# A hybrid SSD and forgetting-attention block: GpSimd's two-input operations on VectorE, h's forms from a float32 copy, a later softplus chain, long output-gate steps, closing sums in PSUM

## The chip, the cores and the metric

The kernel runs on one core of a Trainium2 chip. The core has a matrix engine (TensorE, PE in the profile; PEld are its weight loads), three engines for elementwise work (VectorE or DVE, ScalarE or ACT, GpSimd or POOL), and SyncE (SP), whose queue issues the DMAs here. SBUF is the on-chip memory, PSUM the accumulators that matmuls write (8 banks of 128 x 512 float32). The metric is the device time of one execution in microseconds; a kernel's time is the median of several runs.

## The reference

One decoder layer on x of 1024 tokens by 1024 channels, all float32. c is turned into shift, scale and gate; h is the modulated RMS norm of x; one projection of h gives everything that follows. A Mamba-2 branch (16 heads, chunks of 128 tokens) and a forgetting-attention branch (8 heads of 128) run side by side:

```python
ada = jax.nn.silu(c) @ w_ada + b_ada
shift, scale, gate = jnp.split(ada, 3, axis=-1)
h = _rmsnorm(x, norm_w) * (1.0 + scale[:, None, :]) + shift[:, None, :]
proj = jnp.einsum("bsd,de->bse", h, w_in)
z_ssm, xbc, dt_raw, q, k, v, z_att, f_logit, g_logit = jnp.split(proj, offsets, axis=-1)
y_ssm = _ssd_branch(z_ssm, xbc, dt_raw, conv_w, conv_b, dt_bias, a_log, d_skip, ssm_norm_w)
y_att = _fox_branch(q, k, v, z_att, f_logit, b_f)
g_ssm, g_att = jnp.split(jax.nn.sigmoid(g_logit + b_gate), N_BRANCHES, axis=-1)
merged = g_ssm * (y_ssm @ w_proj_ssm) + g_att * (y_att @ w_proj_att)
x = x + gate[:, None, :] * (merged @ w_out)
return _rmsnorm(x, final_norm_w)
```

`_ssd_branch` runs a causal convolution over 4 tokens and a silu on xbc, takes dt = softplus(dt_raw + dt_bias), and computes the SSD recurrence chunk by chunk. `_fox_branch` is causal softmax attention with a bias from the running sum of log sigmoid(f_logit + b_f), times silu(z_att).

## The kernel before

**Precision.** Every float32 operand of a matmul is split in two: `hi`, its rounding to the type `fp32r`, made by ScalarE, and `lo = raw - hi`, made by a subtraction on GpSimd or VectorE (`split`, L101). A product is three matmuls: hi x hi, hi x lo, lo x hi. `unit` (L87) loads a piece of 128 x 512 weights into a raw tile (tag `wr`, 4 buffers) and splits it into `wh` and `wl` (5 buffers each). GpSimd is the default for the subtraction; a call can name VectorE. Both the cast and the subtraction read the raw tile, which is free for the next load when both are done.

**Strassen products.** Large products of 2 x 2 blocks take seven block products instead of eight (Winograd's form; the products are numbered 1 to 7). Sums of weight blocks are called s1, s2, s4; sums of blocks of h or of the branch outputs are the forms. After each product the block sums x, u2, u3, u4 are built from the PSUM result by adds on VectorE.

**Stages, in the order of the program.** A planner orders the instructions of each engine from the program's order, from priorities and from a model of the machine; each engine then runs its own list in that order, and so does SP with its DMAs.

1. Start (L202 to L326): x and w_ada are loaded; `ada_cols` forms the modulation, `h_half` (L298) transposes x, modulates it (`xa`, L305) and splits it into `hh` and `hl`, held as 8 tiles of 128 x 1024 each. The first three gate slabs (`FIRST`) are multiplied as h comes in.
2. Forms of h (L435): `v_slab(0)` gives the first values and the raw dt and f (`tmp`, a tile of the scratch tag `ev`, 4 buffers of 128 x 1028). `t_forms(k)` for k = 0 to 3 rebuilds h blocks as hh + hl (L440, two on each engine), takes four differences (L441 to L444) and splits them into the tiles tha, tla, thb, tlb. Then `gate_slab(3)`, the softplus chain `dt_chain` (L363) and the prefix sums `ssm_sums` (L401).
3. Pairs (L616): 19 pairs of 128-column slabs, each a Strassen product `c_pair` (L459): 4 raw weight tiles, 4 sums, 7 splits (four into wh and wl, three into `sh` and `sl`), 84 matmuls, 6 adds, and the evacuation of four results by kind: `gate_out` (tanh on ScalarE), `silu_out` (tanh, then a VectorE product), `conv_out` (L528: five VectorE passes over 128 x 1024 for each slab). The table `WPREP` says before which pair the block sums of the closing weights (`w_sums`, L575, stored to DRAM as `ws_scr`) and the output gate's steps (`out_gate`, L548, and `gate_sum`) are done. `out_gate` accumulates w_gate times c into `gb`, one of the `ev` tiles, 256 columns at a time.
4. SSD (L630 to L794): for four groups of four heads, eight chunks each, `ssd_half` (L671) builds the masked decays (`ab`, L686, then `m4`), xd and xe (x times dt, times the decay), the state `st32` with its split `sn`, and the output ys. The list `FILL` puts projections (`v_slab`, `qk_spill`) between as filling for TensorE.
5. Attention (L956 to L1070): for each head `attend` (L993), at high priority, beside `qk_slab` of the next head. GpSimd masks the bias (L1004) and scales the probabilities (L1021). `EARLY` names products of the SSM projection that are done behind heads 6 and 7 (`early`, L924).
6. Closing (L1077 to L1173): the remaining products of the SSM projection (`ps`), seven of the attention projection (`pa`), seven of the output projection (`o`), four tiles each, in the orders `OSSM`, `OATT`, `OOUT`, which are the same. `post` (L866) takes each PSUM tile: in `ps` and `pa` it makes 7 VectorE adds per tile over the seven products, and calls `done` when a block result is complete. In `o`, `pre` (`out_pre`, L1124) adds partial sums to the residual on GpSimd instead. `prod_c` (L897) and `mms` (L1154) issue the matmuls; `bank` hands out PSUM banks, 3 of the tag `mm` and 5 of `pp`. `WV` and `WVI` name the closing weight units that VectorE splits.

GpSimd does most splits, half of L440, two sums in each `w_sums` (L588, L589) and half its products with the gate (L581), xe (L703), the sum of squares (L778), one difference per tile in the closing forms (L861, L1096), the merge of the branches (L1109), the residual sums (L1126), a product with the final weight (L1139), and the powers for the norms.

## Time and profile before

| | |
|---|---|
| median of 3 runs | 1287.4 us (1284.27 to 1290.71) |
| profiled execution, its own time | 1286.09 us |
| its span (first to last instruction) | 1284.4 us |
| mean granted TensorE clock | 0.974 |
| ACT busy | 594.8 us (46%) |
| bytes moved by DMA | 219.70 MB |

In the views below an engine's busy time is the union of its instructions' records. Records of consecutive instructions overlap a little, since an engine's pipe takes the next one in before the last one is out; matmul records overlap their successors by nearly half. A row of the grouped views reads: line, engine, operation, output and inputs by the program's names, partitions x elements, count, then busy us, mean ns of one, idle time of the engine just before, and what ended that idle time. The table by stage cuts the span where the program passes from one stage to the next: 75 the end of the first slabs, 131 the first products of pairs in full, 545 the SSD, 760 mainly attention, 1066 the closing.

### The profile page before, as it was taken

The numbers are of one execution on the slowest core, as the hardware profiler recorded it, in microseconds if no ns is written. First come the engines' busy times: TensorE is split into PE (matmuls) and PEld (weight loads), VectorE is DVE, ScalarE is ACT, GpSimd is POOL, SyncE is SP. The second block draws the span as 40 slices with busy tenths as digits, with TensorE's granted clock in tenths as the row PEclk, the third lists the DMA queues.
The fourth block names the chain that finished last, engine by engine and source line by source line (L and its number), as shares of the span: only waits on it lengthen the run. The fifth ranks groups of instructions, "written<-read, shape, count | busy, mean of one in ns | idle before, by whom it ended". The sixth has DMA issues, their size and how long they took to land. (4 is left out here: it accounts for less than half of the span.)

```text
span 1284.4 us, 18783 instructions
## 1 busy us (share of the span) xinstructions
PE 1183.9 (92%) x6206; PEld 988.8 (77%) x6206; DVE 963.1 (75%) x1618; ACT 594.8 (46%) x1194; POOL 776.1 (60%) x644
## 2 busy tenths in 40 slices
PE   4897899999978999999988999999999999999896
PEld 3686688777766788799778888888887787878685
DVE  6979767787799566348689764545667968999997
ACT  5443324242423232477667733444456553444354
POOL 3258465474755476448887966435446635587666
PEclk9998899998989999999999999999999999999999
DMA  8422443624556566654565558623236619766143
GB/s 346 158 100 98 160 123 124 213 64 167 188 185 216 175 211 228 223 177 148 188 200 163 173 191 296 210 87 116 74 127 210 201 55 328 224 188 193 52 116 145
DMA packets 104126, 219.70 MB, mean 171 GB/s; under 512 B 11818, under 2 KB 19420, under 8 KB 103004
## 3 DMA queue, kind: packets, MB, share of 16 engines
q1 hardware_dynamic: 104028, 218.50, 51.5%
q8 instruction: 49, 0.80, 0.3%
q14 instruction: 49, 0.40, 0.1%
HBM read 154.85 MB, written 63.61 MB: 170 GB/s over the span
## 5 line engine op out<-in xcount | busy, mean ns | idle before, releaser
L103 POOL TENSOR_TENSOR wl<-wr,wh 128x512 fp32r<-128x512 f32 (+1 forms) x188 | 281.5, 1508 | 135.7 <-ACT wh L102 130.7
L102 ACT CAST wh<-wr 128x512 fp32r<-128x512 f32 (+1 forms) x214 | 129.8, 618 | 158.4 <-DMA wr<-w_c 53.7
L103 POOL TENSOR_TENSOR sl<-sr,sh 128x512 fp32r<-128x512 f32 x57 | 91.0, 1603 | 78.8 <-ACT sh L102 65.7
L115 PE MATMUL mm<-hh,wh 128*128 128x512 f32 x288 | 115.9, 407 | 4.3 <-ACT wh L102 1.9
L116 PE MATMUL mm<-hl,wh 128*128 128x512 f32 x288 | 116.7, 405 | 3.0 <-DVE hl L307 3.0
L117 PE MATMUL mm<-hh,wl 128*128 128x512 f32 x288 | 116.3, 405 | 0.0
L102 ACT CAST sh<-sr 128x512 fp32r<-128x512 f32 x57 | 34.1, 619 | 96.6 <-DVE sr L478 77.0
L140 PE MATMUL mm<-wh,hh 128*128 128x256 f32 (+1 forms) x256 | 74.9, 294 | 3.8 <-DVE tmp L348 3.8
L141 PE MATMUL mm<-wl,hh 128*128 128x256 f32 (+1 forms) x256 | 74.8, 293 | 0.0
L142 PE MATMUL mm<-wh,hl 128*128 128x256 f32 (+1 forms) x256 | 74.4, 292 | 0.0
L1018 ACT ACTIVATE pr<-pr,sm 128x1024 f32<-128x1024 f32 (+3 forms) x64 | 49.9, 780 | 50.4 <-DVE sm L1017 42.4
L1021 POOL TENSOR_SCALAR pr<-pr,sm 128x1024 f32<-128x1024 f32 (+3 forms) x64 | 48.6, 762 | 34.7 <-DVE sm L1020 30.2
L1013 DVE CUSTOM_DVE_ANT_0 pr<-lg,fb 128x512 f32<-128x512 f32 (+1 forms) x96 | 51.5, 551 | 23.5 <-PE lg L1012 14.0
L115 PEld LDWEIGHTS mm<-hh,wh 128*128 128x128 f32 x288 | 55.1, 193 | 15.6 <-ACT wh L102 2.4
L116 PEld LDWEIGHTS mm<-hl,wh 128*128 128x128 f32 x288 | 55.3, 192 | 14.7 <-DVE hl L307 3.9
L1004 POOL TENSOR_SCALAR_AFFINE_SELECT fb<-fb 128x128 f32<-128x128 f32 x64 | 21.9, 344 | 72.1 <-DVE sm L1013 57.3
L117 PEld LDWEIGHTS mm<-hh,wl 128*128 128x128 f32 x288 | 55.2, 192 | 10.8
L1037 DVE TENSOR_TENSOR ptl<-tp,pth 128x512 fp32r<-128x512 f32 (+1 forms) x80 | 50.1, 632 | 15.9 <-ACT pth L1036 15.5
L1036 ACT CAST pth<-tp 128x512 fp32r<-128x512 f32 (+1 forms) x80 | 42.3, 543 | 41.5 <-PE tp L1033 32.4
L683 ACT ACTIVATE ab<-ab,acs 128x128 f32<-128x128 f32 x128 | 41.1, 391 | 31.7 <-DMA ab<-a_scr 28.1
L140 PEld LDWEIGHTS mm<-wh,hh 128*128 128x128 f32 x256 | 49.5, 194 | 4.7 <-DVE tmp L348 4.5
L103 POOL TENSOR_TENSOR m<-ab,m 128x512 fp32r<-128x512 f32 x32 | 46.7, 1462 | 7.1 <-ACT m L102 4.7
(393 smaller groups left out, 3972.6 us busy)
## 6 DMA issues: line engine op xcount, KB each, us to landing
wr<-w_c SPq DMA_DIRECT2D x116, 256.0 KB, 3.5
wa<-w_ada SPq DMA_DIRECT2D x8, 1024.0 KB, 11.4
g_scr<-gt SPq DMA_DIRECT2D x16, 512.0 KB, 4.0
ab<-a_scr SPq DMA_DIRECT2D x32, 256.0 KB, 3.7
gt<-g_scr SPq DMA_DIRECT2D x32, 256.0 KB, 3.0
wr<-w_ps SPq DMA_DIRECT2D x28, 256.0 KB, 2.9
wr<-w_pa SPq DMA_DIRECT2D x28, 256.0 KB, 3.1
wr<-so SPq DMA_DIRECT2D x28, 256.0 KB, 2.6
```

Source lines behind the costliest of these rows:

```text
L102: A.copy(out=hi[:, :n], in_=raw[:, :n])
L103: eng.tensor_tensor(out=lo[:, :n], in0=raw[:, :n], in1=f32(hi[:, :n]), op=ALU.subtract)
L115: PE.matmul(ps, lhsT=hi[:, cs], rhs=xh[k][:, hs], start=(k == 0), stop=False)
L116: PE.matmul(ps, lhsT=hi[:, cs], rhs=xl[k][:, hs], start=False, stop=False)
L117: PE.matmul(ps, lhsT=lo[:, cs], rhs=xh[k][:, hs], start=False, stop=(k == 7))
L140: PE.matmul(o, lhsT=xh[k][:, ts], rhs=hi[:, cs], start=(k == 0), stop=False)
L141: PE.matmul(o, lhsT=xh[k][:, ts], rhs=lo[:, cs], start=False, stop=False)
L142: PE.matmul(o, lhsT=xl[k][:, ts], rhs=hi[:, cs], start=False, stop=(k == 7))
L1013: V.tensor_tensor_reduce(out=pr[:, n0:n1], in0=lg[:, :n1 - n0], in1=fb[:, n0:n1], op0=ALU.add, op1=ALU.min, scale=1.0, scalar=BIG, accum_o ...
L1018: A.activation(out=pr[:, :n], in_=pr[:, :n], func=AF.Exp, scale=-1.0, bias=sm[:, 0:1], accum_out=sm[:, 1:2])
L1021: G.tensor_scalar(out=pr[:, :n], in0=pr[:, :n], scalar1=sm[:, 1:2], scalar2=0.5, op0=ALU.mult, op1=ALU.mult)
L1037: V.tensor_tensor(out=ptl[:, :w], in0=tp[:, :w], in1=f32(pth[:, :w]), op=ALU.subtract)
```

## The change

Five edits, made together:

- `split` and `unit` default to VectorE, and every other two-input operation of GpSimd is written for VectorE: L581, L588, L589, L703, L778, L861, L1096, L1109, L1139. GpSimd keeps the masks, the single-input scaling L1021 and the powers. `WV` and `WVI` go, the three orders become one `ORDER`, and `w_sums("ps", 0)` moves from before pair 0 to before pair 1.
- `h_half` stores xa in float32 to DRAM (`h_scr`); `t_forms` loads its four blocks from there instead of adding hh and hl. The odd k use four buffers of the tag `sh`. `gate_slab(3)` goes ahead of the forms.
- The raw dt and f are stored to DRAM (`d_scr`) and loaded before pair 2, where `dt_chain` now runs; the prefix sums (`f_sums`, split off, and `ssm_sums`) come before pair 5.
- `out_gate` takes two rows of w_gate over all 1024 columns at a time instead of 256 columns over eight rows.
- In the closing, products accumulate in PSUM onto the bank of an earlier one (`ONTO`: 2 onto 1, 7 and 4 onto 6, 3 onto 5), and `held` keeps those banks. `out_pre` goes. In `early`, products 1 and 2 are done tile by tile.

```diff
-    def split(raw, hi, lo, n, eng=G):
+    def split(raw, hi, lo, n, eng=V):
         A.copy(out=hi[:, :n], in_=raw[:, :n])
         eng.tensor_tensor(out=lo[:, :n], in0=raw[:, :n], in1=f32(hi[:, :n]), op=ALU.subtract)
...
             A.activation(out=xa, in_=tp, func=AF.Identity, scale=av[:, k:k + 1], bias=sv[:, k:k + 1])
+            SP.dma_start(out=h_scr[k][:, fs], in_=xa)
             A.copy(out=hh[k][:, fs], in_=xa)
...
-            b11, b12, b21, b22 = (pe_tile() for _ in range(4))
+            b11, b12, b21, b22 = (pe_tile() if k % 2 == 0 else pa.tile([P, 512], F32, tag="sh", bufs=SB[1], name="sb")
+                                  for _ in range(4))
-            for b, kk, hs, eng in ((b11, k, lo, V), (b12, k, hi, G), (b22, k + 4, hi, G), (b21, k + 4, lo, V)):
-                eng.tensor_tensor(out=b, in0=f32(hh[kk][:, hs]), in1=f32(hl[kk][:, hs]), op=ALU.add)
+            for b, kk, hs in ((b12, k, hi), (b11, k, lo), (b22, k + 4, hi), (b21, k + 4, lo)):
+                SP.dma_start(out=b, in_=h_scr[kk][:, hs])
...
-            for hf in range(2):
-                wa = ev("wga")[:, :1024].rearrange("p (k c) -> p k c", k=4)
-                SP.dma_start(out=wa, in_=t["w_gate"][g, hf])
-                for kk in range(4):
...
+            for k in (2 * g, 2 * g + 1):
+                wa = ev("wga")[:, :D]
+                SP.dma_start(out=wa, in_=t["w_gate"][k])
+                if k == 0:
+                    V.tensor_scalar(out=gb[:, :D], in0=wa, scalar1=cols[:, k:k + 1], scalar2=None, op0=ALU.mult)
+                else:
+                    V.scalar_tensor_tensor(out=gb[:, :D], in0=wa, scalar=cols[:, k:k + 1], in1=gb[:, :D],
+                                           op0=ALU.mult, op1=ALU.add)
...
         v_slab(0, dtf)
+        SP.dma_start(out=d_scr, in_=tmp[:, 0:192])
+        gate_slab(3)
         for k in range(4):
             t_forms(k)
-        gate_slab(3)
-        dt_chain(dtf, tmp)
-        ssm_sums()
         gb = None
         for n, (sa, sb) in enumerate(PAIRS):
+            if n == 2:
+                tmp = ev("tmp")
+                SP.dma_start(out=tmp[:, 0:192], in_=d_scr)
+                dt_chain(tmp[:, 0:192].rearrange("p (c n) -> p c n", n=24), tmp)
+            if n == 5:
+                f_sums()
+                ssm_sums()
...
-                    G.tensor_tensor(out=h4(xe), in0=h4(xd), in1=hb4(dec), op=ALU.mult)
+                    V.tensor_tensor(out=h4(xe), in0=h4(xd), in1=hb4(dec), op=ALU.mult)
...
-                        G.tensor_tensor(out=sacc[:, hs], in0=sacc[:, hs], in1=zt, op=ALU.add)
+                        V.tensor_tensor(out=sacc[:, hs], in0=sacc[:, hs], in1=zt, op=ALU.add)
...
+    ONTO = {2: 1, 7: 6, 4: 6, 3: 5}
+
+    def post(i, p, ps, x, held, done):
         if i == 1:
             x[p] = fin_tile("x1", 4)
             A.copy(out=x[p], in_=ps)
+            held[1, p] = ps
         elif i == 6:
-            V.tensor_tensor(out=x[p], in0=ps, in1=x[p], op=ALU.add)
...
+            V.tensor_tensor(out=ps, in0=ps, in1=x[p], op=ALU.add)
+            A.copy(out=x[p], in_=ps)
+            held[6, p] = ps
+        elif i == 7:
+            if (6, p) not in held:
+                V.tensor_tensor(out=ps, in0=ps, in1=x[p], op=ALU.add)
+                held[6, p] = ps
+            held["u3", p] = fin_tile("u3", 4)
+            A.copy(out=held["u3", p], in_=ps)
+        elif i == 5:
+            u3 = held.pop(("u3", p))
+            V.tensor_tensor(out=u3, in0=ps, in1=u3, op=ALU.add)
+            V.tensor_tensor(out=ps, in0=ps, in1=x[p], op=ALU.add)
+            held[5, p] = ps
+            done(1, 1, p, u3)
         else:
-            if not pre:
-                V.tensor_tensor(out=ps, in0=ps, in1=u3[p] if i == 4 else x[p], op=ALU.add)
             done(*RESULT[i], p, ps)
+    def prod_bank(i, p, held):
+
+        ps = held.get((ONTO.get(i), p))
+        return (bank(), True) if ps is None else (ps, False)
...
-                PE.matmul(ps, lhsT=hi[:, c], rhs=bf[k][0], start=(k == 0), stop=False)
+                PE.matmul(ps, lhsT=hi[:, c], rhs=bf[k][0], start=(new and k == 0), stop=False, skip_group_check=True)
...
+        for p in range(4):
+            mine = {}
+            for i in js:
+                prod_c(i, "ps", fs[i], sx, mine, done, p)
...
-            G.tensor_tensor(out=m, in0=m, in1=gt, op=ALU.add)
+            V.tensor_tensor(out=m, in0=m, in1=gt, op=ALU.add)
...
-        def out_pre(hf, tk, p, st):
-            r = rt[4 * tk + p, hf]
-            G.tensor_tensor(out=r, in0=r, in1=st, op=ALU.add)
```

More of the change, by code (lines that the diff above doesn't have):

```diff
@@ L169, in build @@
     m_scr = {}
+    h_scr = [dram.tile([P, S], F32, name=f"h_scr{k}") for k in range(NK)]
+    d_scr = dram.tile([P, 192], F32, name="d_scr")
     z_scr = [dram.tile([P, S], F32, name=f"z_scr{j}") for j in range(8)]
@@ L909, in loaded @@
+                PE.matmul(ps, lhsT=hi[:, c], rhs=bf[k][1], start=False, stop=False, skip_group_check=True)
+                PE.matmul(ps, lhsT=lo[:, c], rhs=bf[k][0], start=False, stop=(k == 3), skip_group_check=True)
+            post(i, p, ps, x, held, done)
     def loaded(tag, src):
@@ L920, in g_in, with early @@
         return gt
-    sx, su3 = {}, {}
-    def early(i):
-        fs = []
+    sx, held = {}, {}
+    def early(js):
         def piece(j, hs):
@@ L1064, in build @@
                 qkt = qk_slab(h + 1)
[L1065 to L1067 removed]
+            if h in EARLY:
+                early(EARLY[h])
+                if 1 in EARLY[h]:
                     ub = b_quads(us_scr, (12, 22))
```

172 lines of the change are left out of this document (70 added, 102 removed).

## The prediction

> **What bounds the kernel now.** I read the page's totals first, then a table by stage, then what one kind of instruction costs alone and beside GpSimd, and last the waits.
>
> ```profile
> PE 1183.9 (92%) x6206; PEld 988.8 (77%) x6206; DVE 963.1 (75%) x1618; ACT 594.8 (46%) x1194; POOL 776.1 (60%) x644
> ```
> ```profile
> 160.00:192.00 32.00, 32.00 (x141) 25.97 (x140) 21.64 (x23) 9.97 (x17) 20.34 (x13) 1.00 0.41 124
> ```
> ```profile
> 0.00:75.00 75.00, 52.01 (x232) 39.91 (x233) 54.68 (x122) 37.49 (x61) 19.19 (x24) 0.98 0.57 216
> 75.00:131.00 56.00, 45.37 (x263) 40.26 (x261) 53.82 (x57) 21.00 (x42) 44.59 (x28) 0.94 0.34 113
> 131.00:261.00 130.00, 124.79 (x520) 99.19 (x521) 97.58 (x129) 46.04 (x80) 69.97 (x47) 0.96 0.47 155
> 261.00:545.00 284.00, 264.19 (x1106) 210.68 (x1105) 202.90 (x259) 94.68 (x164) 174.31 (x116) 0.96 0.56 186
> 545.00:760.00 215.00, 200.86 (x1543) 182.71 (x1542) 163.55 (x331) 149.79 (x371) 164.59 (x152) 0.98 0.56 173
> 760.00:960.00 200.00, 199.37 (x1143) 173.24 (x1142) 101.74 (x281) 89.84 (x179) 97.90 (x114) 1.00 0.46 156
> 960.00:1066.00 106.00, 98.04 (x564) 83.50 (x564) 80.54 (x193) 59.31 (x122) 54.94 (x64) 0.97 0.49 161
> 1066.00:1187.00 121.00, 117.98 (x507) 94.70 (x506) 118.98 (x139) 52.15 (x91) 87.83 (x57) 1.00 0.73 237
> 1187.00:1284.40 97.40, 81.30 (x342) 64.62 (x340) 89.35 (x114) 44.45 (x91) 62.76 (x44) 0.96 0.33 105
> ```
>
> Columns: window, length, then busy time (and instructions) of PE, PEld, DVE, ACT, POOL, the clock granted to TensorE, DMA share and rate. TensorE (PE) bounds the kernel: packed, it does 141 full-width matmuls in 32 us, 0.227 us each. No edit removes a matmul, so only time in which PE stands can be won. By count times 0.227, PE needs 118 of the 130 us of 131:261 (12 lost), 251 of 284 in 261:545 (33 lost), 115 of 121 and 78 of 97.4 in the closing (6 and 19 lost). In the mixed stages I take length less busy time: 23 us at the start, 10.6 in 75:131 (the Strassen forms of h), 14 in 545:760 (the SSD), 8 in 960:1066. Some 125 us are open; 760:960 holds nothing.
>
> Why does PE stand? The suspect is something that VectorE (DVE) and GpSimd (POOL) share:
>
> ```profile
> L103 POOL TENSOR_TENSOR wl<-wr,wh x188: 1260/1319/2421, 13.8 to 1246.6; 128x512 fp32r<-128x512 f32 x184, 128x560 fp32r<-128x560 f32 x4
> L103 DVE TENSOR_TENSOR xr<-xd,xr x32: 409/796/1517, 561.1 to 749.4; 128x256 fp32r<-128x256 f32 x32
> L103 DVE TENSOR_TENSOR bl<-b,bh x32: 676/1179/1831, 1066.2 to 1168.8; 128x512 fp32r<-128x512 f32 x32
> L504 DVE TENSOR_TENSOR pe<-pp,pe x12: 678/682/692, 187.4 to 490.3; 128x512 f32<-128x512 f32 x12
> L541 DVE SCALAR_TENSOR_TENSOR cv<-xp,cols,cv x30: 1268/1276/2319, 182.3 to 367.3; 128x1024 f32<-128x1024 f32 x30
> ```
> ```profile
> 133.83 0.68 DVE L477 TENSOR_TENSOR sr<-wr 128x512 f32<-128x512 f32 x1
> 134.43 0.35 DVE L379 SCALAR_TENSOR_TENSOR tmp<-tmp 128x192 f32<-128x192 f32 x1
> ```
>
> Durations are least/median/most in ns. A subtraction with both inputs in SBUF takes 0.68 us on DVE at best, 1.18 at the median, 1.83 at worst; the addition with one input in PSUM (L504) never leaves 0.68 to 0.69. So DVE isn't slow: its operations with two SBUF inputs and POOL's operations take turns. POOL's own subtraction takes 1.26 us at best. In the two timeline rows DVE starts the next instruction 0.60 us after a 128x512 one, 0.08 before its record ends. I use 0.61 us per 128x512, 0.34 per 128x256 (0.409 less 0.07), 1.20 per 128x1024.
>
> **The change part by part.** First, all two-input work to DVE. DVE's load per stage must stay under PE's need. The SSD stage is the tightest:
>
> ```profile
> L103 POOL TENSOR_TENSOR m<-ab,m 128x512 fp32r<-128x512 f32 x32 | 46.7, 1462 | 7.1 <-ACT m L102 4.7 <-issue 1.9
> L103 POOL TENSOR_TENSOR wl<-wr,wh 128x512 fp32r<-128x512 f32 x24 | 33.0, 1391 | 6.3 <-ACT wh L102 5.9
> L103 POOL TENSOR_TENSOR xr<-xe,xr 128x256 fp32r<-128x256 f32 x28 | 24.7, 885 | 10.1 <-ACT xr L102 9.7
> L103 POOL TENSOR_TENSOR sn<-st,sn 64x256 fp32r<-64x256 f32 x28 | 23.5, 841 | 7.6 <-ACT sn L102 5.7
> L703 POOL TENSOR_TENSOR xe<-xd,dec 128x256 f32<-128x256 f32 x28 | 22.7, 810 | 20.0 <-DVE xd L700 19.4
> L778 POOL TENSOR_TENSOR sacc<-sacc,zt 128x512 f32<-128x512 f32 x12 | 16.4, 1365 | 1.9 <-ACT zt L777 1.5
> ```
> ```profile
> L686 DVE TENSOR_TENSOR ab<-ab,cb 128x512 f32<-128x512 f32 x32 | 33.5, 1051 | 15.1 <-ACT ab L685 12.5 <-POOL sn L103 2.3
> L103 DVE TENSOR_TENSOR xr<-xd,xr 128x256 fp32r<-128x256 f32 x32 | 28.2, 884 | 12.1 <-ACT xr L102 12.0
> L773 DVE TENSOR_TENSOR ys<-ys,zt 128x512 f32<-128x512 f32 x15 | 15.4, 1042 | 0.0
> L772 DVE SCALAR_TENSOR_TENSOR ys<-xs,dskip,ys 128x512 f32<-128x512 f32 x16 | 15.3, 993 | 0.1
> ```
>
> These are groups of 545:760: busy us, mean ns, idle before and what ended it. Moved: 68 x 0.61 + 84 x 0.34 = 70 us. Freed from DVE's stretched groups, by mean less least: 32 x 0.37 + 32 x 0.475 + 15 x 0.36 + 16 x 0.31 = 37 us. DVE goes from 163.6 to 163.6 - 37 + 70 = 197 of 215 us, 92%. At first sight that is worse. But what the two engines share is as full today: POOL's 152 operations (68 x 1.26 and 84 x at most 0.81) take 154 us of it, DVE's 95 with two SBUF inputs 63 x 0.61 + 32 x 0.34 = 49, together 203. The chain xd, xe, xr, sn gets shorter (0.34 for 0.81 to 0.885, three times a chunk), the one queue longer. Bounds: 14 us won (all of PE's idle time) or 44 lost (DVE no busier than today's 76%: 197/0.76 = 259). The nearest row is the stage itself, as full as before: I take 0.
>
> In the pairs, each `c_pair` gives DVE 4 sums, 6 adds and now 7 splits: 17 x 0.61 = 10.4 us beside 84 x 0.227 = 19.1 us of PE. A conv pair adds 2 x (4 x 1.20 and one shorter step) = 11, a silu pair 2.4, `w_sums` 2.4, the softplus chain some 6 (25 small operations, at most as the L379 row). Pairs 1 to 5, which hold three conv pairs, that chain, the sums and three `w_sums`, need 23.8 + 18.8 + 23.8 + 12.8 + 23.4 = 103 us of DVE beside 96 of PE: of the 12 us lost in 131:261 I count 4 back. Later pairs need 13 to 21, mean 17, and what they wait for today is this:
>
> ```profile
> SPq L89 <- POOL wl L103: 97.8, 55, 11.7
> SPq L579 <- POOL wl L103: 71.7, 30, 7.2
> SPq L462 <- POOL wl L103: 53.6, 24, 7.7
> ```
> ```profile
> DVE sr L477 <- DMA wr<-w_c: 30.4, 8, 5.4
> ```
> ```profile
> PE mm L495 <- ACT gt L186: 11.2, 2, 7.3
> PE mm L495 <- DVE zt L525: 6.8, 1, 6.8
> ```
>
> (Who waited for whom: total us, times, longest.) The weight loads on SP's queue wait for a raw tile until POOL's split has read it; DVE then waits 30.4 us for those loads, and PE stands. A split of 0.61 for 1.3 us or more returns the tile earlier. The two PE stops of 7 us lie in the pairs with the output gate, where DVE works through conv and gate steps beside POOL. The long gate steps themselves are 8 x 1.20 = 9.6 us for 32 x 0.34 = 11: nearly nothing, but each of the scratch tiles that loads and evacuations share is held by one operation instead of four. I take 14 of the 33 us of 261:545 (bounds: 6 lost, 28 won).
>
> The forms from a float32 copy: per k 4 additions go, 4 subtractions and 4 splits stay, all on DVE, 32 x 0.61 = 19.5 us.
>
> ```profile
> L440 DVE TENSOR_TENSOR pe<-hh,hl x8: 693/1757/1805, 75.5 to 118.8; 128x512 f32<-128x512 f32 x8
> L495 PE MATMUL mm<-hh,wh x60: 387/394/485, 120.1 to 520.7; 128*128 128x512 f32 x60
> ```
> ```profile
> gt<-g_scr SPq DMA_DIRECT2D x32, 256.0 KB, 3.0
> ```
>
> The price is 16 stores and 16 loads of 256 KB on SP's queue and a landing of about 3 us each way: the last quarter of h can be read back some 6 us after it is formed, near 81. Until 75 + 38 = 113 PE has `v_slab(0)` and `gate_slab(3)`, which now stands ahead (45.4 busy less the pair's 7 after 120). DVE's 57 operations, with POOL's 28 and without the 16 additions, are 69 x 0.61 = 42 us at most. So PE meets the first pair (first matmul at 120.1 today) without most of its 10.6 idle us: -10. The softplus chain's wait in the next stage is in the 4 there. If a store held up the loads behind it on SP, up to 6 us return.
>
> Closing sums in PSUM: in the two projections `post` drops from 7 VectorE adds a tile to 3, so 24 x 0.61 = 15 us go (three products of `ps` are early), and ACT gets two more PSUM copies a tile. The 16 additions of POOL L1126 go altogether. New waits: product 2 writes the bank that ACT copies, 7 and 4 that of product 6; all of PE queues behind, but four products (48 x 0.227 = 11 us) lie between. In `early` they follow directly: about 1 us for each of four tiles, under the matmuls of attention; uncovered, 4 us lost.
>
> ```profile
> 1066.00:1187.00 121.00, 59.19 (x50) 56.68 (x36) 1.00 0.73 237
> 1187.00:1284.40 97.40, 52.00 (x45) 7.84 (x5) 0.96 0.33 105
> ```
> ```profile
> 1273.42 0.40 PE L1158 MATMUL pp<-wh,bl 128*128 128x512 f32 x1
> ```
>
> These are the splits (L103) alone, DVE and POOL. DVE's first 50 cost 59.2 us for 50 x 0.61 = 31. With 28 freed, 57 x 0.61 = 35 moved here and 15 dropped, DVE needs 111 of 121 us at most instead of 119; in the last stage 89.4 - 25 + 12 (44 less the 16 and 8 powers) = 77 of 97.4. PE's stops (6, and 19 less the tail of 11 after its last matmul) shrink by 4 and 5, the tail by 1. In 960:1066 the lighter DVE gives 3 (0 to 8). At the start six splits more on DVE stand against less stretching: 0, within 4.
>
> Sum: -10 - 4 - 14 + 0 - 3 - 4 - 5 - 1 = -41. The profiled run took 1286.1 us (span 1284.4 and 1.7 around it), 1.3 below the median of 1287.4: 1245 there, and 1246 as a median.
>
> A rule of the Trainium skill speaks against the change: "GPSIMD Engine Reference", section "Engine selection", has two-input elementwise work about 2x slower on GpSimd than on VectorE. By that ratio alone half of POOL's time would return on DVE, which is the second rival below. The trace agrees on the ratio in the clear (1.26 for 0.61), but POOL's total holds mutual waiting as well, and DVE's total too.
>
> **The rivals.** The SSD becomes DVE-bound (the other side). Splits wait for ACT's rounding (the xr row: 12.0 us idle for 32); on POOL's queue such waits cost nothing, on DVE they hold all behind them, also the PSUM reads that free PE's banks. At a 70% share the stage takes 197/0.70 = 281, 66 more: 1246 + 66 = 1312. It makes the kernel slower below 197/(215 + 48) = 75%. For it speaks today's 76%; against it the 98% of 1066:1187. Chance 0.12.
>
> Half of POOL's time returns: DVE needs 963 + 776/2 - 15 = 1336 us, about 1340 in all. The clear durations speak against it; 0.02.
>
> The loads stay late: SP's queue and its raw tiles, not POOL, set the pace, the pairs give nothing, only forms, attention and closing do: 1287 - 23 = 1264 (1258 to 1280). There are still four raw tiles; 0.18.
>
> PE nearly packed: 261:545 returns 28, the SSD 10: 1246 - 24 = 1222; 0.15.
>
> It doesn't do what it says: one in-order queue loses in the pairs and the SSD what the closing wins, 1281 to 1293; 0.08.
>
> **The numbers.** My forecast (1230 to 1258) has 0.45. About 0.5% (6.4 us) can be told from no change. Faster 0.45 + 0.18 + 0.15 = 0.78, same 0.08, slower 0.14. The range 1214 to 1288 leaves out the slower cases and the best of the packed one.
>
> **What would show it.** Right: splits on DVE at 0.68 throughout, POOL's total a small part of 776, DVE no busier in all than now; the first pair's matmuls near 113 instead of 120; no 7 us stop at the gate; 545:760 within 10 us of 215 with DVE over 88%; some 208 us for the closing's 218. Wrong: an SSD stage over 240, or splits that stay over 1 us without POOL.

## The result, and the profile after

The changed kernel takes 1243.3 us (median of 4 runs, 1242.33 to 1245.01) for 1287.4 before: the ratio is 0.966 (95% interval 0.963 to 0.969). The forecast was 1246. The profiled execution took 1242.6 us, its span 1240.9.

The totals of the page after, and the most frequent split:

```profile
PE 1167.6 (94%) x6206; PEld 981.7 (79%) x6206; DVE 1001.8 (81%) x2026; ACT 604.6 (49%) x1214; POOL 88.0 (7%) x152
...
L99 DVE TENSOR_TENSOR wl<-wr,wh 128x512 fp32r<-128x512 f32 (+1 forms) x214 | 146.1, 689 | 18.9 <-ACT wh L98 18.4
```

GpSimd went from 776 us to 88, and VectorE got busier by only 39 us, although it runs 408 instructions more: its own operations are no longer stretched. The view of one tile shows that for a split of the closing, which had 676/1179/1831 ns (least, median, most) before:

```profile
L99 DVE TENSOR_TENSOR bl<-b,bh x32: 678/683/694, 1040.5 to 1136.7; 128x512 fp32r<-128x512 f32 x32
```

For the stages I cut both traces at the same TensorE instructions, so that a cut means the same in both: first product of `v_slab(0)`, first and last product of the pairs, first and last product of the attention, first and last of the output projection. Columns as in the prediction: window, length, busy us (instructions) of PE, PEld, DVE, ACT, POOL, granted clock, DMA share, GB/s. Before:

```profile
0.00:75.90 75.90, 52.91 (x236) 40.63 (x237) 55.48 (x123) 38.39 (x63) 19.44 (x25) 0.98 0.56 214
75.90:120.10 44.20, 36.90 (x227) 33.70 (x226) 42.23 (x42) 16.61 (x33) 36.65 (x23) 0.92 0.36 121
120.10:541.30 421.20, 392.84 (x1629) 312.13 (x1628) 310.39 (x400) 142.28 (x246) 251.97 (x167) 0.96 0.52 172
541.30:781.70 240.40, 226.26 (x1673) 204.12 (x1672) 166.60 (x336) 160.88 (x386) 179.16 (x163) 0.99 0.59 185
781.70:1060.90 279.20, 271.13 (x1583) 235.25 (x1581) 177.95 (x464) 138.77 (x285) 138.27 (x168) 0.99 0.44 147
1060.90:1188.10 127.20, 123.66 (x532) 99.23 (x532) 122.24 (x144) 54.39 (x94) 87.83 (x57) 1.00 0.73 236
1188.10:1273.40 85.30, 79.78 (x336) 63.76 (x335) 83.50 (x103) 39.18 (x82) 60.71 (x41) 0.98 0.28 85
1273.40:1284.40 11.00, 0.42 (x2) 0.00 (x0) 4.75 (x9) 4.25 (x10) 2.05 (x4) 0.76 0.69 255
```

The same for the changed kernel:

```profile
0.00:72.70 72.70, 53.15 (x236) 41.34 (x237) 51.75 (x132) 38.45 (x63) 6.13 (x15) 0.95 0.73 281
72.70:112.20 39.50, 37.45 (x248) 34.88 (x247) 30.17 (x56) 20.53 (x39) 0.00 (x0) 1.00 0.64 217
112.20:499.70 387.50, 375.56 (x1608) 303.73 (x1607) 336.30 (x534) 139.31 (x240) 0.00 (x0) 0.98 0.56 190
499.70:742.60 242.90, 228.18 (x1695) 204.25 (x1695) 208.77 (x496) 159.71 (x386) 1.65 (x1) 0.99 0.56 181
742.60:1034.60 292.00, 278.23 (x1596) 241.16 (x1596) 198.18 (x508) 142.81 (x291) 75.51 (x128) 0.98 0.43 145
1034.60:1154.40 119.80, 117.08 (x496) 93.47 (x495) 107.46 (x177) 56.38 (x101) 0.00 (x0) 0.99 0.73 246
1154.40:1232.90 78.50, 77.50 (x336) 62.82 (x335) 66.02 (x120) 44.62 (x93) 3.59 (x6) 1.00 0.30 95
1232.90:1240.90 8.00, 0.42 (x2) 0.00 (x0) 3.20 (x7) 2.82 (x6) 1.10 (x2) 0.78 0.75 284
```

Some products changed their stage: the counts of PE say how many (21 from the pairs to the forms, where `gate_slab(3)` now stands ahead, though with the first edit alone the same 21 move without that; 22 from the attention to the SSD; 36 from the projections to the attention, so that the attention's is 14 net, 13 by the records). I take them out at the prediction's 0.227 us each. The table compares the rest with the prediction's terms.

| stage | length after less before, us | of it moved products | left | predicted |
|---|---|---|---|---|
| start | -3.2 | 0 | -3.2 | 0 |
| forms | -4.7 | +4.8 | -9.5 | -10 |
| pairs | -33.7 | -4.8 | -28.9 | -18 |
| SSD, up to the first product of the attention | +2.5 | +5.0 | -2.5 | 0 |
| attention | +12.8 | +3.2 | +9.6 | -3 |
| projections ps and pa | -7.4 | -8.2 | +0.8 | -4 |
| output projection | -6.8 | 0 | -6.8 | -5 |
| tail | -3.0 | 0 | -3.0 | -1 |
| sum | -43.5 | 0 | -43.5 | -41 |

The sum came out, two of its terms didn't: the pairs gave 11 us more, and the attention took 10 where 3 were to be won. That these two misses cancel, so that the total lies within 3 us of the forecast, is luck. In the pairs the view of who waited for whom shows what went. After, for the pairs, all that TensorE waited for by name:

```profile
PE mm L496 <- DVE zt L526: 11.9, 2, 6.8
```

The 11.2 us of `gt` are gone, but the stop of 6.8 us behind `zt` is there, and a second one. Over the whole trace VectorE waits less for weights (30.4 us with stops up to 5.4 before):

```profile
DVE sr L478 <- DMA wr<-w_c: 10.5, 8, 2.4
```

### The profile page after: what moved, and what is told of

Read it like the earlier page. It is cut to its first block, busy times and chain, and to the rows that moved or that the text cites. A ratio compares the mean times of both kernels' runs of the same rounds, so it can differ in the third digit from the quotient of the medians.

```text
span 1240.9 us, 18420 instructions
## 1 busy us (share of the span) xinstructions
PE 1167.6 (94%) x6206; PEld 981.7 (79%) x6206; DVE 1001.8 (81%) x2026; ACT 604.6 (49%) x1214; POOL 88.0 (7%) x152
## 4 chain that ended last, share of the span: by engine, by line
PE 60%; DVE 19%; DMA 11%; issue 5%; ACT 3%; SPq 1%; POOL 0%; DVEq 0%; POOLq 0%; ACTq 0%
PE pp L497 4%; PE pp L498 4%; PE pp L496 4%; PE pv L1057 4%; PE lg L1026 3%; PE mm L112 3%; PE mm L113 3%; PE mm L111 3%; PE mm L496 3%; PE mm L498 3%; PE mm L497 3%; DMA ab<-a_scr 2%; PE tp L1047 2%; DVE wl L99 2%; PE mm L911 2%
## 5 line engine op out<-in xcount | busy, mean ns | idle before, releaser
L99 DVE TENSOR_TENSOR wl<-wr,wh 128x512 fp32r<-128x512 f32 (+1 forms) x214 | 146.1, 689 | 18.9 <-ACT wh L98 18.4
L1050 ACT CAST pth<-tp 128x512 fp32r<-128x512 f32 (+1 forms) x80 | 42.4, 542 | 54.7 <-PE tp L1047 45.9
L112 PEld LDWEIGHTS mm<-hl,wh 128*128 128x128 f32 x288 | 55.2, 192 | 13.4 <-DVE hl L306 3.2
L111 PEld LDWEIGHTS mm<-hh,wh 128*128 128x128 f32 x288 | 54.4, 191 | 10.5 <-ACT hh L305 0.8
L1051 DVE TENSOR_TENSOR ptl<-tp,pth 128x512 fp32r<-128x512 f32 (+1 forms) x80 | 49.9, 631 | 11.4 <-ACT pth L1050 11.1
L1035 POOL TENSOR_SCALAR pr<-pr,sm 128x1024 f32<-128x1024 f32 (+3 forms) x64 | 51.9, 812 | 87.1 <-DVE sm L1034 73.7
L1057 PE MATMUL pv<-pth,vh 128*128 128x256 f32 (+1 forms) x160 | 45.9, 287 | 5.2 <-DVE zg L1060 4.6
L137 PEld LDWEIGHTS mm<-wl,hh 128*128 128x128 f32 x256 | 48.2, 189 | 0.2
## 6 DMA issues: line engine op xcount, KB each, us to landing
wa<-w_ada SPq DMA_DIRECT2D x8, 1024.0 KB, 11.4
```

The source lines that it names most:

```text
L99: eng.tensor_tensor(out=lo[:, :n], in0=raw[:, :n], in1=f32(hi[:, :n]), op=ALU.subtract)
L111: PE.matmul(ps, lhsT=hi[:, cs], rhs=xh[k][:, hs], start=(k == 0), stop=False)
L112: PE.matmul(ps, lhsT=hi[:, cs], rhs=xl[k][:, hs], start=False, stop=False)
L137: PE.matmul(o, lhsT=xh[k][:, ts], rhs=lo[:, cs], start=False, stop=False)
L1057: PE.matmul(pv[:, o0:256], lhsT=x[kb // 4][:, kb % 4, vs], rhs=y[:, d:d + m], start=(kb == 0 and i == 0), stop=(kb == 2 * qq + 1 and i == 2))
```

## The experiments

All of them are the kernel before or the changed kernel with one edit, except two at the end. Times are medians; the changed kernel is at 1243.3, the kernel before at 1286 to 1288 in the same sessions. From one kernel to the next, stages whose code is the same differ by up to 3 us, as the planner orders the whole program anew; only more than that is read as an effect.

**The first edit alone.** The kernel before with every two-input operation and split on VectorE:

```diff
-    def split(raw, hi, lo, n, eng=G):
+    def split(raw, hi, lo, n, eng=V):
...
-                    G.tensor_tensor(out=h4(xe), in0=h4(xd), in1=hb4(dec), op=ALU.mult)
+                    V.tensor_tensor(out=h4(xe), in0=h4(xd), in1=hb4(dec), op=ALU.mult)
```

> The kernel before with the first edit alone: every two-input operation of GpSimd and every split on VectorE; forms by additions, softplus chain, gate steps and closing sums as before. If the gain comes from ending the turn-taking of GpSimd and VectorE, most of the 44 us is here: about 1255 (1248 to 1262), the pairs as short as in the changed kernel (about 388 us from the first pair's first matmul to the last's), the closing some 8 us longer than there. Rival, the other four edits carry it and the move alone only shifts load: 1270 to 1290, with the pairs still over 410.

Measured: 1249.1 us (1246.46 to 1251.06; 0.970 of before, interval 0.967 to 0.973, and so for the others). So 38 of the 44 us belong to this edit. The forms, the pairs, the SSD and the attention in its table by stage:

```profile
73.30:110.70 37.40, 37.40 (x248) 35.04 (x247) 36.47 (x69) 18.71 (x38) 0.00 (x0) 1.00 0.50 172
110.70:509.00 398.30, 378.98 (x1608) 301.20 (x1607) 344.35 (x562) 141.29 (x243) 0.00 (x0) 0.98 0.52 179
509.00:746.40 237.40, 228.48 (x1695) 205.26 (x1694) 208.32 (x496) 159.78 (x386) 1.65 (x1) 1.00 0.57 185
746.40:1024.60 278.20, 266.57 (x1559) 230.78 (x1560) 197.32 (x506) 139.69 (x285) 78.04 (x128) 0.99 0.43 150
```

In the forms TensorE is busy 37.40 of 37.40 us: without any float32 copy, with all 16 additions on VectorE, nothing is left to win there. The pairs are at 398.3 with 1608 products, which is 18 us less than before by the same correction, but not at the 388 that was expected. The SSD is 8 us shorter than before by that correction (3.0 in length and 22 products more), where the changed kernel has 2.5. None of the edits undone alone below brings that back (the SSD takes 242 to 245 us in all of those kernels), so its cause stays open.

**The splits back on GpSimd**, everything else of the change kept:

```diff
-    def split(raw, hi, lo, n, eng=V):
+    def split(raw, hi, lo, n, eng=G):
```

> The changed kernel with GpSimd as the default engine of the splits again (weights, sums, decays, states, attention's loads); the closing's block splits and all other moved operations stay on VectorE. Turn-taking: VectorE's two-SBUF operations stretch again (conv step L541 of before from 1.27 to 1.5 or more on the mean), and 25 to 35 us come back: 1268 to 1280. Rival, the splits are not what mattered but the other moves and edits: within 8 us of 1243.

Measured: 1276.5 us (1273.28 to 1280.79; 0.992 of before, 0.989 to 0.994): 33 us come back. A weight's split takes 1.32 us on GpSimd (median), and VectorE's conv steps, 1.28 us in the changed kernel, take 1.72 (median). The pairs in the table by stage:

```profile
120.50:530.50 410.00, 380.06 (x1608) 306.15 (x1608) 312.50 (x404) 138.18 (x240) 206.71 (x131) 0.96 0.52 180
```

410.0 us for 387.5, though neither VectorE (312.5) nor GpSimd (206.7) is near 410. This fits turn-taking, but a slower split would lengthen the pairs too; hence the next one. How much of the 33 us belongs to each of the two is not separated by any run.

**Work that nobody waits for.** The changed kernel with 100 subtractions on GpSimd, on a tile of their own, during the projections. No engine needs their result; one VectorE operation has to wait 3.4 us until the first of them has read its tile.

```diff
+        junk = frp.tile([P, 512], F32, tag="junk", bufs=1, name="junk")
+        G.tensor_tensor(out=junk, in0=b[11][0], in1=b[11][0], op=ALU.subtract)
+        for _ in range(100):
+            G.tensor_tensor(out=junk, in0=junk, in1=junk, op=ALU.subtract)
```

> The changed kernel plus 100 subtractions on GpSimd over a tile of their own in the closing; nobody waits for them. Turn-taking: GpSimd is busy for 130 to 175 us of the closing's 206, VectorE's splits there go from 0.68 to 1.1 us or more, and the closing grows by 7 to 20 us: 1250 to 1263. Rival, what hurt was GpSimd's own slow splits that others wait for (raw tiles held, late loads): the splits may stretch, but the closing stays within 3 us: 1241 to 1247.

Measured: 1301.9 us (1299.61 to 1303.84; 1.011 of before, 1.008 to 1.014): 58 us more, three times the most that was expected. The two kinds of operation by tile, and the projections (119.8 us in the changed kernel):

```profile
L1100 POOL TENSOR_TENSOR junk<-junk x100: 1038/1368/1592, 1042.1 to 1184.3; 128x512 f32<-128x512 f32 x100
```
```profile
L99 DVE TENSOR_TENSOR bl<-b,bh x32: 676/1523/1527, 1048.5 to 1201.2; 128x512 fp32r<-128x512 f32 x32
```
```profile
1038.00:1215.20 177.20, 133.87 (x496) 102.27 (x496) 173.44 (x172) 56.53 (x101) 136.75 (x101) 0.87 0.51 163
```

The same split that takes 683 ns in the changed kernel takes 1523 beside GpSimd. The stage is 57 us longer with the same 496 products, and VectorE is at 173 of 177 us. A few consecutive rows of the timeline show whom it hits:

```profile
1078.99 11.16 POOL L1100 TENSOR_TENSOR junk<-junk 128x512 f32<-128x512 f32 x8
...
1079.38 0.68 DVE L890 TENSOR_TENSOR u<-pp,u 128x512 f32<-128x512 f32 x1
...
1080.58 1.44 DVE L99 TENSOR_TENSOR bl<-b,bh 128x512 fp32r<-128x512 f32 x1
1081.95 4.41 DVE L99 TENSOR_TENSOR wl<-wr,wh 128x512 fp32r<-128x512 f32 x3
```

GpSimd works without a pause. The addition with an input in PSUM takes 0.68 us; the four splits, with both inputs in SBUF, take 1.4 to 1.5 each, one for each GpSimd operation (11.16/8 = 1.40). So turn-taking is shown, by work whose results nobody uses. GpSimd's own operation takes 1.04 us while VectorE reads PSUM and 1.37 beside an operation with two SBUF inputs (least and median above); in its timeline the next one starts 0.08 later, so 1.12 and 1.45 from start to start. The Trainium skill says the same in "SBUF — State Buffer", section "SBUF: two separate sides": a VectorE instruction with two SBUF inputs and a GpSimd instruction that reads SBUF exclude each other for whole instructions, and the one that comes second blocks fully. The trace agrees on who is hit. By full exclusion a pair would take 1.12 and 0.61, together 1.73 us; the trace has 1.45, so a part of each overlaps.

**The attention's splits on GpSimd**, since the attention had got longer:

```diff
-                    split(qt, hi, lo, S)
+                    split(qt, hi, lo, S, G)
...
-                split(vt, vh[g], vl[g], 4)
+                split(vt, vh[g], vl[g], 4, G)
```

(and the weights of `qk_slab` likewise.)

> The changed kernel with attention's own splits (its slab weights, the reloaded q, k and v) on GpSimd again. Attention is the one stage that the change made longer (279 to 292 us between the same matmuls). If those splits, on VectorE's one queue, hold up the softmax chain, attention falls back to about 281 and the time to about 1233. Rival, the order that the planner gave the matmuls, or another filling, not VectorE's queue: attention stays at 289 to 295, time within 3 of 1243. Second rival, GpSimd's splits now take turns with VectorE and delay the chain further: 1247 or more.

Measured: 1250.9 us (1248.6 to 1252.46; 0.971, 0.968 to 0.975). The attention is at 298.8 us for 292.0: taking splits out of VectorE's queue doesn't help, and the time is the second rival's. A split of v takes 2.46 us on GpSimd (mean of 8) for 1.25 on VectorE, and VectorE's scalings of the SSM output take 1.54 beside it for 1.28. Which of the two makes the stage longer isn't shown.

**The forms by additions**, the second edit undone:

```diff
-            SP.dma_start(out=h_scr[k][:, fs], in_=xa)
...
-                SP.dma_start(out=b, in_=h_scr[kk][:, hs])
+                V.tensor_tensor(out=b, in0=f32(hh[kk][:, hs]), in1=f32(hl[kk][:, hs]), op=ALU.add)
```

> The changed kernel with the forms of h made by 16 additions on VectorE again instead of the trip through DRAM. The changed kernel waits 2.2 us in the forms stage; VectorE has 30 of 39.5 us there. Hidden either way (VectorE has room for 16 x 0.61 = 10 us): first pair within 2 us of 112.2, time 1241 to 1246. Rival, the float32 copy is what freed the forms stage: first pair at 117 or later, 1248 or more.

Measured: 1234.9 us (1230.65 to 1236.89; 0.960 of before, 0.957 to 0.964). Neither theory had this: it is faster than the changed kernel, each of its runs below each of that kernel's. The forms and the attention in its table by stage:

```profile
72.90:111.10 38.20, 37.64 (x248) 35.07 (x247) 38.20 (x71) 20.56 (x39) 0.00 (x0) 1.00 0.34 117
...
741.00:1026.80 285.80, 276.42 (x1595) 239.81 (x1596) 197.43 (x508) 142.76 (x291) 74.87 (x128) 0.98 0.44 149
```

The forms themselves are 1.3 us shorter than with the copy. Most of the span's 5.7 us is in the attention, 285.8 for 292.0, a stage whose code is the same in both. All of it is in the first head: 56.7 us for 62.9 with the same 294 products, while each of the seven later heads agrees within 0.2. It isn't chance between runs: with the copy that head takes 61.3 to 62.9 us in five of these kernels (the changed one, with idle work, short gate steps, the chain early, the closing as before), without it 56.7 here and in the last one below (59.0 with the first edit alone, where the other edits are missing too). In that head the planner put the same instructions in another order, and the timeline shows one place where that costs. VectorE in the changed kernel, in the attention's first head:

```profile
781.96 1.23 DVE L99 TENSOR_TENSOR vl<-vt,vh 128x1024 fp32r<-128x1024 f32 x1 [4.57 <-ACT vh L98]
...
783.17 0.40 DVE L1060 TENSOR_TENSOR zg<-pv,zg 128x256 f32<-128x256 f32 x1
```

And ScalarE there:

```profile
780.88 1.04 ACT L98 CAST vh<-vt 128x1024 fp32r<-128x1024 f32 x1 [3.69 <-DMA vt<-v_scr]
```

A load of v came late; ScalarE's cast waited for it, VectorE's split of v for the cast, and `zg` behind the split; TensorE waited 3.1 us for `zg`. The longest that TensorE waited for by name in the first head, in the changed kernel and then in this one:

```profile
PE pv L1057 <- DVE zg L1060: 3.1, 1, 3.1
```
```profile
PE lg L1025 <- DMA fb<-f_scr: 1.4, 1, 1.4
```

In the kernel with additions the same split finds its cast almost done:

```profile
774.67 1.23 DVE L99 TENSOR_TENSOR vl<-vt,vh 128x1024 fp32r<-128x1024 f32 x1 [0.25 <-ACT vh L98]
...
776.07 0.41 DVE L1059 TENSOR_TENSOR zg<-pv,zg 128x256 f32<-128x256 f32 x1
```

**Short gate steps**, the fourth edit undone, 256 columns over eight rows as before:

```diff
-            for k in (2 * g, 2 * g + 1):
-                wa = ev("wga")[:, :D]
+            for hf in range(2):
+                wa = ev("wga")[:, :1024].rearrange("p (k c) -> p k c", k=4)
...
+                        V.scalar_tensor_tensor(out=gb[:, gc], in0=wa[:, kk, :], scalar=cols[:, k:k + 1],
+                                               in1=gb[:, gc], op0=ALU.mult, op1=ALU.add)
```

> The changed kernel with the output gate in 256-column steps again. With the first edit alone the pairs were 11 us longer than in the changed kernel (398.4 against 387.6). If the gate's steps are the cause (four operations hold each scratch tile, evacuations queue), the pairs grow by 6 to 11 us: 1249 to 1254. Rival, the softplus chain's place is: here within 3 us of 1243.

Measured: 1250.6 us (1247.92 to 1254.21; 0.973, 0.970 to 0.977): the long steps are worth 7 us. The pairs take 396.9 for 387.5. Three views: the steps by tile, then what TensorE waited for in the pairs; first the changed kernel's steps, then this kernel's.

```profile
L558 DVE SCALAR_TENSOR_TENSOR gb<-wga,cols,gb x7: 1271/1273/1277, 352.5 to 381.9; 128x1024 f32<-128x1024 f32 x7
```
```profile
L562 DVE SCALAR_TENSOR_TENSOR gb<-wga,cols,gb x28: 474/482/489, 350.8 to 394.8; 128x256 f32<-128x256 f32 x28
```
```profile
PE mm L496 <- DVE zt L526: 11.9, 2, 7.5
PE pp L571 <- DVE gb L562: 7.9, 1, 7.9
```

The 28 adding steps sum to 13.5 us of records, the 7 long ones to 8.9. And the gate's product, which closes the sum, stops TensorE for 7.9 us behind a step; the changed kernel has no such row.

**The softplus chain at its old place**, ahead of the pairs:

```diff
+        dt_chain(dtf, tmp)
+        f_sums()
+        ssm_sums()
```

> The changed kernel with the softplus chain and the sums ahead of the pairs again. If the chain's place is the cause of the 11 us by which the pairs were longer with the first edit alone, the pairs grow by 6 to 11 us: 1249 to 1254. Rival, the gate's steps are: here within 3 us of 1243.

Measured: 1244.1 us (1241.58 to 1247.18; 0.968, 0.965 to 0.971). The chain's place makes no difference that shows.

**Scaling of the SSM output at other heads.** In the attention's first head VectorE also scales the SSM output (`u_scaled`), six of its eight pieces. They were put behind heads 1 and 2:

```diff
-PREP = (6, 1, 0, 0, 0, 0, 0, 0, 1)
+PREP = (0, 4, 4, 0, 0, 0, 0, 0, 0)
```

> The changed kernel with the eight scalings of the SSD output (L809) after heads 1 and 2 of attention instead of around head 0. Attention's extra idle time of TensorE lies in head 0 (8.4 us there, about none before the change), where VectorE's queue stands 3.8 us for the norm's row and some 5 us for these loads. If that queue is the cause, head 0 has at most 4 us idle and the time falls by 4 to 8: 1235 to 1239. Rival, attention now begins with less filling in hand (SSD's filling is used up), whatever stands in VectorE's queue: 1241 to 1246.

Measured: 1250.8 us (1247.04 to 1251.87; 0.973, 0.969 to 0.976). The theory falls: the attention is 297.0 us long for 292.0. The first head lost its 3.1 us stop and is down to 56.2 us, but the second and third have others behind the softmax, together 6.7 us.

**More filling at the seam.** In the changed kernel TensorE stands between the SSD and the attention, where nothing over 0.5 us stood before (timeline of TensorE):

```profile
737.79 1.05 PE L787 MATMUL sp<-ones,sacc 128*128 128x1 f32 x8 [1.59 <-DVE sacc L781]
740.83 0.38 PE L794 MATMUL sp<-ident,fl 128*8 128x128 f32 x1 [1.99 <-POOL fl L792]
742.61 0.76 PE L1026 MATMUL lg<-kh,qh 128*128 128x512 f32 x1 [1.40 <-DMA fb<-f_scr]
```

```diff
-SPILL = (("q", 0), ("k", 0), ("k", 2), ("k", 4), ("q", 7), ("k", 5), ("k", 6), )
+SPILL = (("q", 0), ("k", 0), ("k", 2), ("k", 4), ("q", 7), ("k", 5), ("k", 6), ("q", 6), )
-FILL = [[], [0, 2], [4, 5, 9], [1, 3, 6, 7, 8]]
+FILL = [[], [0, 2], [4, 5, 9], [1, 3, 6, 7, 8, 10]]
```

> The changed kernel, but the query slab of head 6 is projected among the fillings of the SSD and spilled, instead of during the attention. In the changed kernel TensorE stands 2.0, 2.2 and 1.8 us (together 6.0) between the last state product and the first attention product, where the kernel before has no stop over 0.5 us and 25 us of filling. If the lack of filling at that seam is what attention lost, the 48 products of the slab (48 x 0.227 = 10.9 us) fill it, the seam's stops go, and the time falls by 4 to 6 us, to 1237 to 1239. The rival: the heads that lose the slab then stand by as much, since their own products wait for the softmax; the seam is filled, and the total stays within 2 us of 1243.

Measured: 1243.3 us (1242.8 to 1244.24; 0.966, 0.964 to 0.968). The rival was right. The seam's three stops are gone, the SSD and the attention together take 533.9 us for 534.9, and the fifth head stops instead: TensorE waits in it 5.3 us for the softmax on VectorE, in three stops up to 2.0, where it waited 1.5 in the changed kernel. The heads before and after it lost 24 and 22 of the products that filled them.

**The closing's sums as before**, the fifth edit undone, all on VectorE:

```diff
-            V.tensor_tensor(out=ps, in0=ps, in1=x[p], op=ALU.add)
-            A.copy(out=x[p], in_=ps)
-            held[6, p] = ps
+            V.tensor_tensor(out=x[p], in0=ps, in1=x[p], op=ALU.add)
```

> The changed kernel with the closing's block sums as before (additions of every product by VectorE outside PSUM, residual sums one by one, products 1 and 2 done one after the other behind head 6), all of it on VectorE: the fifth edit undone alone. The prediction's theory: 15 us of VectorE additions that go give 4 us in the projections and 5 us in the last stage; with them back the time is 8 to 11 us longer, 1251 to 1254, the loss in the stage of the output projection above all. The rival: without GpSimd VectorE has room for them beside the matmuls (its share there is 84 to 90%), and the time is within 2 us of 1243.

Measured: 1249.8 us (1248.27 to 1252.27; 0.971, 0.969 to 0.973): 6.5 us more, between the two theories. The closing's three stages:

```profile
1030.60:1153.80 123.20, 122.68 (x532) 99.58 (x531) 117.63 (x196) 53.31 (x92) 0.00 (x0) 1.00 0.70 237
1153.80:1235.60 81.80, 78.21 (x337) 62.70 (x335) 77.89 (x140) 39.77 (x81) 2.25 (x4) 1.00 0.28 88
1235.60:1248.40 12.80, 0.38 (x2) 0.00 (x0) 6.72 (x14) 5.16 (x12) 2.40 (x4) 0.63 0.75 282
```

The sums in PSUM save 3.3 us in the output projection and 4.8 in the tail. In the projections they lose: with the sums as before, 123.2 us less the 36 products (8.2) are 115.0, for 119.8. The last kernel below, with the same sums in the projections, says so too: 123.1 less 8.2 are 114.9, for 121.8 in the kernel with additions. Together the closing gains 3.3; the other half of the 6.5 lies in stages that the edit doesn't touch (pairs +2.6, SSD +2.3), so no more than 3.3 of it is shown to be the edit's.

**Two combinations.** The forms by additions with the filling of the seam (both diffs above):

> The changed kernel with the forms rebuilt by additions on VectorE and head 6's query slab among the SSD's fillings. The forms alone gave 1234.9. If the two gains are at different places they add: 1229 to 1231. If both only remove the same stop in the attention's first head, it is 1233 to 1237.

Measured: 1236.9 us (1234.29 to 1239.95; 0.961, 0.958 to 0.963): no better than the additions alone, as the second expectation has it. The first head is at 54.7 us here and at 55.2 with the filling alone, so both had removed the same stop. Against the filling alone the copy still costs 6.4 us, of which 5 lie before the first pair: TensorE waits there 2.2 us behind the split of h and 2.1 behind `tmp` with the copy, 0.6 behind `tmp` without. And the forms by additions with sums in PSUM only in the output projection:

```diff
-            prod_c(i, "pa", b_form(i, b), sx, held, att_done)
+            prod_c(i, "pa", b_form(i, b), sx, su3, att_done)
...
-                    post(i, tb, ps[tb][0], sx, held, out_done)
+                    post_o(i, tb, ps[tb][0], sx, held, out_done)
```

(`post` is the one of before, `post_o` the changed one.)

> The changed kernel with the forms rebuilt by additions on VectorE (alone 1234.9) and the two projections' block sums outside PSUM as before, on VectorE; only the output projection sums in PSUM. In the changed kernel TensorE stands 4.3 us in four stops at the start of the projections, with those sums as before 0.8 us in one; in the output projection it stands 1.4 us, with the sums as before 4.8, and the tail after its last matmul is 7.9 against 12.8. If the sums in PSUM pay in the output projection alone, this version takes the better of both: 3 to 5 us less than 1234.9, 1230 to 1232. The rival: the stops in the projections hang on where the attention ends and which weights are split then, not on where the sums are made; the time stays at 1233 to 1237. A second rival: two sums more a tile in the projections keep VectorE from the splits of the output projection, 1237 to 1241.

Measured: 1241.4 us (1239.16 to 1244.56; 0.966, 0.963 to 0.968). This is the second rival's case, 0.4 us above its range: the output projection, 78.7 us with the additions alone, takes 87.1, and TensorE waits in it 5.8 us for splits, which VectorE and ScalarE now reach late, for 1.0:

```profile
PE pp L1193 <- DVE bl L99: 3.2, 2, 2.6
PE mm L1190 <- ACT bh L98: 2.6, 1, 2.6
```

So the fastest version is the change without its float32 copy, 1234.9 us.

## Why the prediction was right, and where it was not

**The cause was right.** Operations with two SBUF inputs on VectorE and GpSimd's operations take turns, and the weights' splits are where it hurts: the first edit alone gives 38 us, the splits moved back to GpSimd cost 33, and 100 operations that nobody needs cost 58. How much of the 38 us came from VectorE's stretched operations, and how much from GpSimd's slower splits that held the raw tiles, stays open. The second rival (half of GpSimd's time returns on VectorE) needed 373 us more of VectorE; it was 39, since the 408 added instructions came with the end of the stretching.

**The SSD**, the rival on the other side: VectorE is at 208.8 of 242.9 us, 86%, where I had named 75% as the share below which the kernel gets slower, and the stage lost nothing. My 0 was too low for the first edit, which alone wins 8 us here; over 5 of them are gone in the whole change. The sign "DVE over 88%" was slightly too high. Three others were met: splits at 0.68, GpSimd's total at 88 us, the first pair near 113 (112.2). The closing's 206.3 looks like the 208, but the closing begins 5 us earlier here than in the 218, and 8 us of the difference are products that moved. "DVE no busier in all than now" was wrong by 39 us.

**The pairs were mis-sized: -18 forecast, -28.9 measured.** The first edit gives 18 of it by itself. The step that failed is the one on the gate: "The long gate steps themselves are 8 x 1.20 = 9.6 us for 32 x 0.34 = 11: nearly nothing". The 0.34 was worked out from a split of 256 columns, whose record is 0.41; the record of a gate step is 0.48. That makes the steps' difference 4.6 us by records instead of 1.4 (VectorE is busy 4.6 us longer in the pairs with short steps, 340.9 for 336.3), in a stretch where VectorE works back to back; and the product behind them, which I hadn't listed among the waits, stopped TensorE for 7.9 of the 9.4 us. The softplus chain, part of my -4, is worth nothing. My sign "no 7 us stop at the gate" was wrong: the one behind `zt` stayed at 6.8, for around it VectorE works back to back.

**The forms were right in size and wrong in cause.** I gave 10 us to the whole edit with its float32 copy. VectorE alone, with all additions, gives them (37.40 of 37.40 us busy). The copy saves VectorE some 8 us that TensorE doesn't wait for, and the kernel without it is 8.5 us faster. Of my price for the copy, "If a store held up the loads behind it on SP, up to 6 us return", the wait is there: SP's queue stands 22.8 us, in 11 stops, until ScalarE has written the `xa` that the stores read, and the kernel before has none of it. Which load came late by it isn't shown.

**The attention has the wrong sign: -3 forecast, +9.6 measured.** The step that failed is "In 960:1066 the lighter DVE gives 3", together with "760:960 holds nothing": a stage without idle time could only lose, and I gave that no price. VectorE isn't lighter there (198 us for 178), and what waits for late loads (the split of v behind its cast) stands since then in the queue in front of softmax steps. Of the 9.6, some 4 come with the first edit (278.2 us with 1559 records, for 279.2 with 1583) and 5 to 6 with the copy's edit, all in the first head, by another order of the same instructions. Neither moving the splits, nor the scaling, nor the filling brought them back: the stage, with the SSD where the filling moved, stayed as long or got longer, with its stops at other heads. That the late load costs 3.1 us in this order is shown by the rows; which rule would keep the planner from such an order stays open.

**The closing was right in sum, -9.0 for -10**, and wrong in its parts: the projections gave nothing for the -4, the output projection and the tail 9.8 for the 6. The step that failed is "PE's stops (6, and 19 less the tail of 11 after its last matmul) shrink by 4 and 5", in its first half: with the first edit alone the projections take 124.8 us, 2.4 less than before, and in the whole change, with the sums in PSUM, they are 3 longer than that again, moved products taken out (5 longer, judged by the kernel with the sums as before). The reason stays open. The new waits on a bank, which I priced at nothing, don't show in the rows: TensorE waits there 2.7 us by name, 2.2 of it for splits on VectorE.

**By edits**, each undone alone: forms -8.5 (the edit costs), chain 0.8, gate 7.2, closing 6.5, together 6.0; from the first edit alone to the whole change it is 5.8. These are differences of medians of 4 runs each. Taken instead by the ratios to the kernel before, measured beside each, they are -7.1, 2.8, 9.4 and 6.3, together 11.4, for 5.3. So that they add up isn't shown, nor that no edit hides another; that the copy costs and that the gate's and the closing's edits pay holds both ways.

The rival "the loads stay late" fell: SP still waits for splits (VectorE's now), yet VectorE's wait for weights went from 30.4 us to 10.5.

## What to carry to other kernels

Before moving work by the clock of one operation, compare the least with the median of that operation: where they lie far apart and operations with a PSUM input don't spread, two engines may be taking turns, and one engine with all the work may be faster than two. Operations that nobody needs, put on the other engine, tell it. Undo each edit alone in the end, for a gain of the right size can hide an edit that costs: here one of five cost 6 to 8 us. In a stage where TensorE has no idle time, ask what a change can lose, not what it can win.

## What the runs showed that was not expected

- Beside GpSimd work without pause, VectorE does one operation with two SBUF inputs per GpSimd operation: 1.45 us a pair, for 0.61 alone. The 101 operations made the stage 57.4 us longer, 0.57 us for each; I had expected a third of that at most.
- A stop costs more than its length. Behind the 6.8 us stop that is left in the pairs, products of 512 columns start every 0.43 us, and only from the ninth on every 0.23 (timeline of TensorE in the changed kernel):

```profile
380.80 0.80 PE L496 MATMUL mm<-tha,sh 128*128 128x512 f32 x1 [6.79 <-DVE zt L526]
...
383.10 0.63 PE L498 MATMUL mm<-tha,sl 128*128 128x512 f32 x1
383.52 0.63 PE L496 MATMUL mm<-tha,sh 128*128 128x512 f32 x1
...
384.26 0.39 PE L498 MATMUL mm<-tha,sl 128*128 128x512 f32 x1
384.49 0.40 PE L496 MATMUL mm<-tha,sh 128*128 128x512 f32 x1
```

Eight products take the 3.46 us up to 384.26 instead of 1.8, which is 1.6 more; the prediction priced stops by their length alone. Between kernels it comes out alike: the pairs with short gate steps are 9.4 us longer with 7.9 us more of stops. The Trainium skill has it in "TensorE: Matmul & The Clock Gate", section "What's actually happening": after an idle window of some 3.4 us the clock is halved, and it takes as long a busy one to come back. The rows agree: it takes 3.46 us here. In the projections of the run with idle work, where TensorE was busy 134 of 177 us, the granted clock was 0.87 for 0.99.
